# Where the norm of three feed-forwards is applied, and how SBUF is parted into pools, in a diffusion backbone step

## The chip, the core and the metric

The kernel runs on one core of one Trainium2 chip. The time is the device time of one execution in microseconds (us); lower is better. The core's engines are TensorE (PE, matrix products; PEld is its weight load), VectorE (DVE), ScalarE (ACT), GpSimd (POOL) and SyncE (SP, which issues nearly all transfers). Products accumulate in PSUM, all else lies in SBUF.

## The reference, cut to what matters

Two layers, each with a feed-forward, a mixer (attention with latent keys in layer 0, Fourier mixing in layer 1) and a second feed-forward. So there are four feed-forwards: (layer, position) = (0, 0), (0, 1), (1, 0), (1, 1). Each works on 640 tokens of 1024 features; 512 of them are sample tokens and 128 are prompt tokens, with modulations of their own.

```python
def _rms(x, g):
    y = xf * lax.rsqrt(jnp.mean(xf * xf, axis=-1, keepdims=True) + EPS)
    return (y * g).astype(x.dtype)
def _modulate(h, shift, scale):
    return h * (1 + scale) + shift
def _swiglu(h, wg, wu, wd):
    return (jax.nn.silu(h @ wg) * (h @ wu)) @ wd
...
for l in range(DEPTH):
    m = split(silu(cond) @ w_mod[l] + b_mod[l], 9)
    y = y + 0.5 * m[2] * _swiglu(_modulate(_rms(y, norm_g[l, 0]), m[0], m[1]), ffn_wg[l, 0], ffn_wu[l, 0], ffn_wd[l, 0])
    y = y + m[5] * mixer(_modulate(_rms(y, norm_g[l, 1]), m[3], m[4]))
    y = y + 0.5 * m[8] * _swiglu(_modulate(_rms(y, norm_g[l, 2]), m[6], m[7]), ffn_wg[l, 1], ffn_wu[l, 1], ffn_wd[l, 1])
```

The inner width of a feed-forward is 2816, which is 22 tiles of 128.

## The kernel before, in words

x is kept transposed: features on the 128 partitions (8 tiles d of 128 features, the k-tiles of a product), tokens along the free axis. Tokens are parted into half A (384 sample tokens) and half B (128 sample and 128 prompt tokens). A number is split into a high and a low part, and every product is made in three passes (L295 to L297 in `mm3`: high by high, low by high, high by low). Weights arrive by transfers of 512 KB that SP issues (L97, `raw`), ACT makes the high part (L101, `whi`), POOL the low part (L104, `wlo`, 512 columns at a time); three units of weights are held at once.

A feed-forward (`ffn`) goes over its 22 tiles in chunks of 4, 4, 2, 4, 4, 4. Two tiles at a time, the gate and up products of half A are made for both, then those of half B for both (48 matmuls each: 8 k-tiles, gate and up, three passes), and behind the chunk the down products of half A and of half B add into x (L494). A tile's gate and up products fill a pair of PSUM banks (`bank2`, tile name s); there are two such pairs. All else in PSUM goes through four single banks (`bank`, tile name t).

The norm (`Norm`): as soon as a tile of x is there, its product with the scale is split (`scale`, L171 on ACT and L172 on DVE), so the products can start. Two more columns in half A carry the shift through the products, so half A has 386 columns there. The factor 1/rms is multiplied onto gate and up behind the products (`scaled`, L530 on DVE, twice a tile), and the bias that the two columns gave goes into silu (L539 on ACT) and the product of the two (L540 on DVE). 1/rms itself (`rstd`) is a chain: squares on ACT (L314), their sum over tiles on POOL (L317), the sum over partitions as matmuls with ones (L333), a power on POOL (L343), three or two diagonal tiles on DVE (L350), matmuls that spread it over the partitions (L355), a copy to SBUF on ACT (L359).

The modulations of layer 1 and the last ones of layer 0 are reduced on DVE (L403) while the feed-forwards run; they need the silu of the condition in `crow`, which a transfer (L1246) and ACT (L1247) make ready after the attention. The Fourier mixer needs small tables `fc` (transfer L1019, first used at L1024).

The order of the work is the order in which the Python code emits it, engine by engine. Tasks (`spawn`, `tick`) put chains such as `rstd` and the modulations between the products: a task yields pauses in nanoseconds of PE time, and is emitted further once that much product work was emitted behind it. Memory comes from pools; a new tile waits for the readers of the old one in its place.

## Time and profile before

| | us |
|---|---|
| median of 3 runs | 2341.88 (2341.56 to 2344.65) |
| span of the profiled execution, first to last instruction | 2338.8 |
| PE busy in it | 2291.2 (98%) |
| DVE, POOL, ACT busy | 1522.5, 932.3, 769.6 |

The profiled execution has no time of its own beside its span; the median lies 3.1 us above the span. PE is busy nearly all the time, so the end of the program moves when PE does fewer or shorter matmuls, or when it waits more or less; an engine that is busy 65% of the time matters where PE waits for it.

### The profile page before, as it was taken

What the parts mean: (1) busy time and instruction counts of PE and PEld (TensorE: products, weight loads), DVE (VectorE), ACT (ScalarE), POOL (GpSimd) and SP (SyncE); (2) the same over time, 40 slices, a digit from 0 to 9 for tenths busy, and PEclk for the clock granted to TensorE, in tenths of its full rate; (3) what the DMA queues carried; (4) which work ended last, traced back from release to release, by engine and by line L of the source; (5) the groups of instructions that cost most, each with busy time, mean ns of one, the idle gap of its engine ahead of it and who ended that gap; (6) DMA issues with size and microseconds to landing.
All of it is one profiled execution on the core that took longest, in us unless ns stands there. A gap on an engine that the chain in (4) does not pass through costs nothing.

```text
span 2338.8 us, 38924 instructions
## 1 busy us (share of the span) xinstructions
PE 2291.2 (98%) x15724; PEld 2267.9 (97%) x15724; DVE 1522.5 (65%) x2852; ACT 769.6 (33%) x1601; POOL 932.3 (40%) x759
## 2 busy tenths in 40 slices
PE   8899999999999999999999999999999999999998
PEld 6899999999899999999999999999999999999998
DVE  5977778767677776777677767775356743353434
ACT  4222223253544632222224322222237422232323
POOL 1544434464111344353445543533346433343433
PEclk9999999999999999999999999999999999999999
DMA  8543434421011233344333333433212222221221
GB/s 303 167 135 127 142 121 153 135 81 55 28 42 41 91 100 127 127 136 131 131 127 100 109 127 127 144 121 103 73 51 82 71 75 73 73 76 65 94 65 46
DMA packets 70467, 243.92 MB, mean 104 GB/s; under 512 B 7888, under 2 KB 12688, under 8 KB 70032
## 3 DMA queue, kind: packets, MB, share of 16 engines
q1 hardware_dynamic: 70288, 241.44, 31.0%
q8 instruction: 124, 2.03, 0.4%
q14 instruction: 55, 0.45, 0.1%
HBM read 238.62 MB, written 2.79 MB: 103 GB/s over the span
## 4 chain that ended last, share of the span: by engine, by line
PE 89%; DVE 6%; ACT 3%; DMA 1%; issue 1%; POOL 1%; SPq 0%; POOLq 0%; DVEq 0%; ACTq 0%
PE s L296 17%; PE s L297 17%; PE s L295 17%; PE t L295 12%; PE t L296 11%; PE t L297 11%; DVE junk L403 1%; ACT whi L101 1%; DVE b L540 1%; PE t L861 0%; DVE b L305 0%; ACT p L809 0%; DVE a L305 0%; DVE x L494 0%; DVE p L812 0%
## 5 line engine op out<-in xcount | busy, mean ns | idle before, releaser
L104 POOL TENSOR_TENSOR wlo<-raw,whi 128x512 fp32r<-128x512 f32 x592 | 827.4, 1427 | 1236.8 <-ACT whi L101 1187.8
L101 ACT CAST whi<-raw 128x1024 fp32r<-128x1024 f32 (+1 forms) x303 | 306.3, 1036 | 644.9 <-PE t L296 334.9
L295 PE MATMUL s<-a,whi 128*128 128x386 f32 (+1 forms) x1408 | 478.1, 340 | 4.4 <-DVE b L530 3.3
L297 PE MATMUL s<-a,wlo 128*128 128x386 f32 (+1 forms) x1408 | 478.7, 340 | 0.1
L296 PE MATMUL s<-a,whi 128*128 128x386 f32 (+1 forms) x1408 | 478.5, 340 | 0.0
L295 PE MATMUL s<-b,whi 128*128 128x256 f32 (+1 forms) x1408 | 395.7, 281 | 0.0
L296 PE MATMUL s<-b,whi 128*128 128x256 f32 (+1 forms) x1408 | 395.5, 281 | 0.0
L297 PE MATMUL s<-b,wlo 128*128 128x256 f32 (+1 forms) x1408 | 395.4, 281 | 0.0
L494 DVE SCALAR_TENSOR_TENSOR x<-t,mod,x 128x128 f32<-128x128 f32 (+1 forms) x696 | 277.8, 433 | 160.5 <-PE t L297 157.1
L403 DVE CUSTOM_DVE_ANT_0 junk<-wmt,crow 128x1024 f32<-128x1024 f32 x256 | 372.4, 1455 | 3.5 <-ACT crow L1247 1.0
L295 PE MATMUL t<-a,whi 128*128 128x384 f32 (+1 forms) x968 | 329.8, 341 | 14.3 <-DVE x L494 5.4
L296 PE MATMUL t<-a,whi 128*128 128x384 f32 (+1 forms) x968 | 328.0, 339 | 1.3 <-DVE a L305 1.2
L297 PE MATMUL t<-a,wlo 128*128 128x384 f32 (+1 forms) x968 | 327.2, 338 | 0.0
L295 PEld LDWEIGHTS s<-a,whi 128*128 128x128 f32 x1408 | 266.8, 190 | 5.7 <-issue 4.1
L295 PE MATMUL t<-b,whi 128*128 128x256 f32 x936 | 265.2, 283 | 4.8 <-ACT b L359 2.7
L297 PEld LDWEIGHTS s<-a,wlo 128*128 128x128 f32 x1408 | 266.4, 189 | 2.2 <-issue 1.6
L296 PEld LDWEIGHTS s<-a,whi 128*128 128x128 f32 x1408 | 266.6, 189 | 1.6 <-issue 1.2
L295 PEld LDWEIGHTS s<-b,whi 128*128 128x128 f32 x1408 | 265.6, 189 | 0.0
L296 PEld LDWEIGHTS s<-b,whi 128*128 128x128 f32 x1408 | 265.5, 189 | 0.0
L297 PEld LDWEIGHTS s<-b,wlo 128*128 128x128 f32 x1408 | 265.2, 188 | 0.0
L530 DVE TENSOR_TENSOR a<-s,a 128x384 f32<-128x384 f32 x176 | 89.8, 551 | 266.3 <-ACT gub L526 264.2
L297 PE MATMUL t<-b,wlo 128*128 128x256 f32 x936 | 263.1, 281 | 0.0
(216 smaller groups left out, 3431.3 us busy)
## 6 DMA issues: line engine op xcount, KB each, us to landing
raw<-in_gu SPq DMA_DIRECT2D x176, 512.0 KB, 3.7
wmt<-in_wm SPq DMA_DIRECT2D x134, 512.0 KB, 4.0
raw<-in_dn SPq DMA_DIRECT2D x88, 512.0 KB, 3.7
raw<-in_uq SPq DMA_DIRECT2D x8, 512.0 KB, 3.6
raw<-in_wo SPq DMA_DIRECT2D x8, 512.0 KB, 3.7
raw<-in_fw SPq DMA_DIRECT2D x8, 512.0 KB, 3.7
crow<-in_wm SPq DMA_DIRECT2D x6, 512.0 KB, 5.9
junk<-in_wm SPq DMA_DIRECT2D x4, 512.0 KB, 5.3
```

Of the source, the lines that this page charges most:

```text
L101: nc.scalar.copy(hi[:, c : c + e], raw[:, :e])
L104: eng.tensor_tensor(lo[:, c + o : c + o + w], raw[:, o : o + w], hi[:, c + o : c + o + w].bitcast(F32), op=ALU.subtract,)
L295: mm(out, wh, xh, start=first and i == 0, stop=False)
L296: mm(out, wh, xl, start=False, stop=False)
L297: mm(out, wl, xh, start=False, stop=last and i == end)
L403: nc.vector.tensor_tensor_reduce(self.junk, raw, self.crow[:, c * D : (c + 1) * D], 1.0, 0.0, ALU.mult, ALU.add, self.mod[l][m][:, d, c : ...
L494: self.mark = self.nc.vector.scalar_tensor_tensor(xd, ps[:, cols], gate[:, d, c : c + 1], xd, ALU.mult, ALU.add)
L530: nc.vector.tensor_tensor(t, ps[:, m * 512 : m * 512 + n], r, op=ALU.mult)
L540: nc.vector.scalar_tensor_tensor(g[:, cols], up[:, cols], bias[:, 1, c : c + 1], g[:, cols], ALU.add, ALU.mult)
```

## The change

The last three feed-forwards, (0, 1), (1, 0) and (1, 1), take a norm `PreNorm`: 1/rms is computed first, as soon as x is complete, and x is then normalised, scaled and shifted, and split, before the products. The products have 384 columns in half A, no factor and no bias behind them: silu reads PSUM at once (`gate_up_n`). The matmul that spreads 1/rms over the partitions writes one of the two bank pairs of gate and up (`k.bank2`), and DVE reads the factor from there. The sum over partitions takes the last tile's square by itself, so the matmuls with ones number 65 in place of 50. A normalised tile holds both halves in one piece.

Second, the SBUF pools are kept as two stacks, one on the left and one on the right of SBUF. Each stage closes its pools and opens new ones in the same memory, and a first write there waits for the readers of what lay there. The tiles of the modulations (`crow` among them) and those of the Fourier mixer (`fc` among them) are opened on the right, where the attention's and a feed-forward's tiles lay.

```diff
+class PreNorm:
+    def feed(self, d, H):
...
+        sq = k.add_square(None if d == KT - 1 else self.acc[H], k.xs(d, H), H)
+        self.acc[H] = [self.acc[H], sq] if d == KT - 1 else sq
...
+    def normalise(self, H):
+        k, nc = self.k, self.k.nc
+        r = yield from k.rstd(self.acc[H], H, D, True, *self.pauses[H], False, k.bank2)
+        sh, sc = (k.mod[self.l][3 * self.i + j] for j in range(2))
+        for d in range(KT):
+            while not self.open:
+                yield 200
+            if not H:
+                self.h.append((k.wide(k.hpool, "h"), k.wide(k.hpool, "h")))
+            hi, lo = (t[:, k.cols(H)] for t in self.h[d])
+            t = k.half(H, F32)
+            x = k.xs(d, H)
+            for cols, c in k.parts(H):
+                b = sh[:, d, c : c + 1]
+                nc.vector.scalar_tensor_tensor(t[:, cols], x[:, cols], sc[:, d, c : c + 1], r[:, cols], ALU.mult, ALU.mult)
+                nc.scalar.activation(hi[:, cols], t[:, cols], AF.Identity, bias=b)
+                k.mark = nc.vector.scalar_tensor_tensor(
+                    lo[:, cols], t[:, cols], b, hi[:, cols].bitcast(F32), ALU.add, ALU.subtract
+                )
+            yield 900
...
     def open_phase(self, name):
-        self.phase = self.tc.tile_pool(name=self.name(name), bufs=1)
-        return self.phase.__enter__()
+        return self.open_pool(name, 1, "right")
...
+    def gate_up_n(self, w, h, H, G):
+        nc = self.nc
+        n = NA if H == 0 else NB
+        ps = self.bank2()
...
+        g = self.half(H, F32)
+        nc.scalar.activation(g, ps[:, :n], AF.Silu)
+        nc.vector.tensor_tensor(g, ps[:, 512 : 512 + n], g, op=ALU.mult)
+        self.split(g, *(t[:, self.cols(H)] for t in G))
...
+        def to_ffn(nxt):
+            self.close_pools(len(self.stack["left"]))
+            self.open_ffn()
+            nxt.start()
...
-        nrm, nxt = nxt, Norm(self, 0, 2)
-        nxt.pauses[0] = (7500, 5500)
+        nrm, nxt = nxt, PreNorm(self, 0, 2)
         self.mla(nrm, nxt)
+        to_ffn(nxt)
         mods_on()
         mods_go()
-        nrm, nxt = nxt, Norm(self, 1, 0)
-        self.ffn(0, 1, nrm, nxt)
+        nrm, nxt = nxt, PreNorm(self, 1, 0)
+        nxt.start()
+        self.ffn_n(0, 1, nrm, nxt)
...
+        self.ffn_n(1, 0, nrm, nxt, before_fourier)
+        self.close_pools(3, "right")
+        nrm, nxt = nxt, PreNorm(self, 1, 2)
         self.fourier(nrm, nxt)
+        to_ffn(nxt)
```

What this does to the order, at the three places that matter below. In the changed program L262 to L264 are the three lines of `normalise`, L403 is the square (L314 before), L1381 the silu of `crow` (L1247), L384 to L386 the three passes (L295 to L297), L406 POOL's sum (L317), L422 the matmul with ones (L333), L713 and L714 the silu and product of `gate_up_n`, L492 a reduction (L403), L394 the low part of a split (L305). A name ends in the number of its buffer.

**From the attention to feed-forward (0, 1), on ACT.** Before, the silu of `crow` stood ahead of the first scaled tiles of x:

```order
L304 CAST b_8246<-t_9030 128x128
L1247 ACT_TABLE_LOAD
L1247 ACTIVATE crow_9305<-crow_9305 128x2048
L171 ACTIVATE a_9084<-x_84,mod_7_108 128x384
L101 CAST whi_9034<-raw_9036 128x1024
```

Now it stands behind the squares of half B and behind two of the eight normalised tiles h:

```order
L263 ACTIVATE h_9303<-a_9305,mod_6_98 128x384
L403 ACTIVATE b_9385<-x_80 128x256
L403 ACTIVATE b_9391<-x_81 128x256
L263 ACTIVATE h_9309<-a_9311,mod_6_98 128x384
L403 ACTIVATE b_9397<-x_82 128x256
L101 CAST whi_9251<-raw_9255 128x1024
L1381 ACT_TABLE_LOAD
L1381 ACTIVATE crow_9282<-crow_9282 128x2048
L263 ACTIVATE h_9315<-a_9317,mod_6_98 128x384
L263 ACTIVATE h_9321<-a_9323,mod_6_98 128x384
```

So the third tile of h waits on ACT for the transfer of `crow` and for its silu. That transfer waits, in the changed program, for the last product of the attention's output projection, whose operands lay in its memory.

**From feed-forward (0, 1) to (1, 0), on POOL and PE.** On POOL the last two sums of half B's squares before, behind one unit's four subtractions (x2 stands for two instructions):

```order
L104 TENSOR_TENSOR wlo_13686<-raw_13687,whi_13685 128x512 x2
L104 TENSOR_TENSOR wlo_13686<-raw_13689,whi_13685 128x512 x2
L317 TENSOR_TENSOR b_13904<-b_13904,b_14055 128x256
L317 TENSOR_TENSOR b_13904<-b_13904,b_14085 128x256
L104 TENSOR_TENSOR wlo_14089<-raw_14090,whi_14088 128x512 x2
```

and now the last one:

```order
L406 TENSOR_TENSOR b_13607<-b_13607,b_13723 128x256
L104 TENSOR_TENSOR wlo_13444<-raw_13445,whi_13443 128x512 x2
L104 TENSOR_TENSOR wlo_13444<-raw_13447,whi_13443 128x512 x2
L406 TENSOR_TENSOR b_13607<-b_13607,b_13747 128x256
L104 TENSOR_TENSOR wlo_13780<-raw_13781,whi_13779 128x512 x2
```

POOL's order there is nearly the same. On PE the matmuls with ones that read this sum stood, before, behind the whole first tile (48 matmuls, and three more of the second):

```order
L295 MATMUL s_14182<-a_13708,whi_13685 128x386
L296 MATMUL s_14182<-a_13709,whi_13685 128x386
L297 MATMUL s_14182<-a_13708,wlo_13686 128x386
L333 MATMUL t_14186<-ones,b_13904 128x1 x2
L295 MATMUL s_14182<-a_13708,whi_13685 128x386
```

Now they stand in the first tile, behind 13 of its matmuls:

```order
L384 MATMUL s_13820<-h_13733,whi_13380 128x384
L385 MATMUL s_13820<-h_13734,whi_13380 128x384
L386 MATMUL s_13820<-h_13733,wlo_13381 128x384
L384 MATMUL s_13820<-h_13754,whi_13380 128x384
L422 MATMUL t_13858<-ones,b_13607 128x1
L422 MATMUL t_13858<-ones,b_13771 128x1
L422 MATMUL t_13858<-ones,b_13607 128x1
L422 MATMUL t_13858<-ones,b_13771 128x1
L385 MATMUL s_13820<-h_13755,whi_13380 128x384
```

So PE meets them 38 matmuls earlier.

**The second tile of (1, 0), on DVE.** s_13917 is half B's spread 1/rms in one bank pair, s_13897 the second tile of half A in the other. The 12 rows up to the product (L714) that frees s_13897:

```order
L264 SCALAR_TENSOR_TENSOR h_13755<-b_13948,mod_0_101,h_13754 128x128 x2
L262 SCALAR_TENSOR_TENSOR b_13961<-x_78,mod_1_102,s_13917 128x128 x2
L262 SCALAR_TENSOR_TENSOR b_13974<-x_79,mod_1_102,s_13917 128x128
L264 SCALAR_TENSOR_TENSOR h_13774<-b_13961,mod_0_101,h_13773 128x128 x2
L264 SCALAR_TENSOR_TENSOR h_13797<-b_13974,mod_0_101,h_13796 128x128
L262 SCALAR_TENSOR_TENSOR b_13974<-x_79,mod_1_102,s_13917 128x128
L262 SCALAR_TENSOR_TENSOR b_13988<-x_80,mod_1_102,s_13917 128x128 x2
L264 SCALAR_TENSOR_TENSOR h_13797<-b_13974,mod_0_101,h_13796 128x128
L492 ISA junk_9283,mod_5_106<-wmt_9285,crow_9282 128x1024
L492 ISA mod_5_106 128x1
L264 SCALAR_TENSOR_TENSOR h_13803<-b_13988,mod_0_101,h_13802 128x128 x2
L714 TENSOR_TENSOR a_13998<-s_13897,a_13998 128x384
```

Between the first read of s_13917 and L714 stand 24 such instructions of half B and two reductions. Before, the two L530 that free the second tile's bank pair stood behind the reductions alone:

```order
L305 TENSOR_TENSOR a_14179<-a_14172,a_14178 128x384
L403 ISA junk_9306,mod_5_115<-wmt_9307,crow_9305 128x1024
L403 ISA mod_5_115 128x1
L403 ISA junk_9306,mod_5_115<-wmt_9308,crow_9305 128x1024
L403 ISA mod_5_115 128x1
L530 TENSOR_TENSOR a_14252<-s_14182,a_14112 128x384
```

So the work of 1/rms on half B has moved ahead of the evacuation of the second tile, and it holds a bank pair of its own meanwhile.

## Rows read from the trace of the kernel before

**Rows 1.** The page: span, busy time. Waits of PE: us in total, times, longest.

```profile
span 2338.8 us, 38924 instructions
...
PE 2291.2 (98%) x15724; PEld 2267.9 (97%) x15724; DVE 1522.5 (65%) x2852; ACT 769.6 (33%) x1601; POOL 932.3 (40%) x759
...
PE t L295 <- DVE x L494: 6.3, 8, 1.2
```

**Rows 2.** Timeline of PE: start, duration, matmul; first and last of stretches.

```profile
803.95 0.34 PE L295 MATMUL t<-a,whi 128*128 128x384 f32 x1
...
812.33 0.28 PE L295 MATMUL t<-b,whi 128*128 128x256 f32 x1
...
824.05 0.34 PE L295 MATMUL s<-a,whi 128*128 128x386 f32 x1
...
827.57 0.34 PE L297 MATMUL s<-a,wlo 128*128 128x386 f32 x1
...
1303.56 0.34 PE L296 MATMUL s<-a,whi 128*128 128x386 f32 x1
...
1309.60 0.34 PE L297 MATMUL s<-a,wlo 128*128 128x386 f32 x1
```

**Rows 3.** Timeline of PE: matmuls behind a wait; in brackets idle time and releaser.

```profile
580.86 0.39 PE L295 MATMUL t<-b,whi 128*128 128x256 f32 x1 [2.73 <-ACT b L359]
...
831.05 0.71 PE L355 MATMUL t<-dg,ones 128*128 128x128 f32 x4 [1.33 <-DVE dg L350]
```

**Rows 4.** Windows: busy time of engines; the column behind POOL is the granted clock.

```profile
575.00:580.00 5.00, 2.38 (x12) 2.06 (x12) 4.70 (x13) 2.49 (x6) 0.19 (x1) 1.00 0.18 59
580.00:585.00 5.00, 4.14 (x19) 4.14 (x20) 3.93 (x10) 2.62 (x8) 0.00 (x0) 0.66 0.09 26
...
820.00:840.00 20.00, 18.66 (x110) 18.16 (x110) 16.80 (x33) 10.35 (x28) 13.75 (x17) 1.00 0.16 54
```

**Rows 5.** Timeline of SP and ACT, around the transfer and silu of crow.

```profile
798.31 0.33 SPq L1246 DMA_DIRECT2D crow<-in_crow  x1
...
802.85 1.28 ACT L1247 ACT_TABLE_LOAD   x1 [1.27 <-DMA crow<-in_crow]
804.14 1.92 ACT L1247 ACTIVATE crow<-crow 128x2048 f32<-128x2048 f32 x1
805.96 0.60 ACT L171 ACTIVATE a<-x,mod 128x384 fp32r<-128x384 f32 x1
```

**Rows 6.** Timeline of POOL from feed-forward (0, 1) to (1, 0).

```profile
1293.84 0.74 POOL L317 TENSOR_TENSOR b<-b,b 128x256 f32<-128x256 f32 x1 [1.79 <-ACT b L314]
1294.71 5.15 POOL L104 TENSOR_TENSOR wlo<-raw,whi 128x512 fp32r<-128x512 f32 x4
1299.82 2.67 POOL L317 TENSOR_TENSOR b<-b,b 128x256 f32<-128x256 f32 x2
```

**Rows 7.** Timeline of PE there: first matmul of the first tile; the matmuls with ones.

```profile
1293.22 0.34 PE L295 MATMUL s<-a,whi 128*128 128x386 f32 x1
...
1302.94 0.50 PE L333 MATMUL t<-ones,b 128*128 128x1 f32 x4
```

**Rows 8.** Timeline of DVE there.

```profile
1293.13 0.65 DVE L172 SCALAR_TENSOR_TENSOR b<-x,mod,b 128x128 fp32r<-128x128 f32 x2
...
1295.92 4.83 DVE L172 SCALAR_TENSOR_TENSOR b<-x,mod,b 128x128 fp32r<-128x128 f32 x4 [1.10 <-ACT b L171]
1300.68 1.21 DVE L403 CUSTOM_DVE_ANT_0 junk<-wmt,crow 128x1024 f32<-128x1024 f32 x1
...
1302.80 0.56 DVE L530 TENSOR_TENSOR a<-s,a 128x384 f32<-128x384 f32 x1 [0.90 <-ACT gub L526]
```

**Rows 9.** The tile fc: its transfer, its first use, and the time to landing.

```profile
L1024 PE MATMUL t<-mod,fc x8: 170/256/256, 1764.9 to 1765.6; 128*128 128x8 f32 x8
...
L1019 SPq DMA_DIRECT2D fc<-in_dftx x1: 327/327/327, 1616.0 to 1616.0; - x1
...
DMA to landing us min/median/max: 3.5/3.5/3.5
```

More of the change, by code (lines that the diff above doesn't have):

```diff
@@ L208, in r, with __init__, finish, later @@
         return self.task[H].join()
+class PreNorm:
+    def __init__(self, k, l, i):
+        self.k, self.l, self.i = k, l, i
+        self.h = []
+        self.acc = [None, None]
+        self.task = [None, None]
+        self.feeds = [None, None]
+        self.open = False
+        self.started = False
+        self.pauses = [(3500, 3500), (4500, 4500)]
+    def feed(self, d, H):
+        k = self.k
+        if not self.started:
+            self.started = True
+            k.need_mod((self.l, 3 * self.i), (self.l, 3 * self.i + 1))
+        sq = k.add_square(None if d == KT - 1 else self.acc[H], k.xs(d, H), H)
+        self.acc[H] = [self.acc[H], sq] if d == KT - 1 else sq
+    def finish(self, H):
+        self.task[H] = self.k.spawn(self.normalise(H))
+    def later(self, H, pace=300):
+        self.feeds[H] = self.k.spawn(self.feed_all(H, pace))
+    def feed_all(self, H, pace):
+        for d in range(KT):
+            yield pace
+            self.feed(d, H)
+        self.finish(H)
+    def start(self):
+        self.open = True
+    def normalise(self, H):
+        k, nc = self.k, self.k.nc
+        r = yield from k.rstd(self.acc[H], H, D, True, *self.pauses[H], False, k.bank2)
+        sh, sc = (k.mod[self.l][3 * self.i + j] for j in range(2))
+        for d in range(KT):
+            while not self.open:
[13 more added lines that the diff above has]
+            yield 900
+    def get(self, H):
+        if self.feeds[H] is not None:
+            self.feeds[H].join()
+        self.task[H].join()
+        return [tuple(t[:, self.k.cols(H)] for t in h) for h in self.h]
 class Kern:
@@ L320, in add_square, with rstd @@
         return acc
[L322 removed]
+    def rstd(self, acc, H, dim, bcast=True, lag=6000, gap=4200, copy=True, bank=None):
         nc = self.nc
@@ L352, in rstd @@
         yield min(gap, 1500)
-        ps = self.bank()
+        ps = (bank or self.bank)()
         for j in range(nb):
@@ L608, in ffn, with ffn_n @@
             self.down(wds, gB, 1, gate, nxt if last else None)
+            u.prefetch(nf // 2)
+    def gate_up_n(self, w, h, H, G):
+        nc = self.nc
+        n = NA if H == 0 else NB
+        ps = self.bank2()
+        wh, wl = w
+        for k in range(KT):
+            for m in range(2):
+                s = slice((m * KT + k) * P, (m * KT + k + 1) * P)
+                self.mm3(ps[:, m * 512 : m * 512 + n], [((wh[:, s], wl[:, s]), h[k])], n, k == 0, k == KT - 1)
+                if (k, m) != (KT - 1, 1):
+                    self.tick(self.last)
+        g = self.half(H, F32)
+        nc.scalar.activation(g, ps[:, :n], AF.Silu)
+        nc.vector.tensor_tensor(g, ps[:, 512 : 512 + n], g, op=ALU.mult)
+        self.split(g, *(t[:, self.cols(H)] for t in G))
+        self.tick(self.last)
+    def ffn_n(self, l, i, nrm, nxt, before_last=None):
+        gm = (l, 2 if i == 0 else 8)
+        gate = self.mod[l][gm[1]]
+        u = self.units
+        for ch, nf in enumerate(CHUNKS):
+            last = ch == len(CHUNKS) - 1
+            gs = []
+            for q in range(0, nf, 2):
+                if last and q == nf - 2:
+                    self.mods_stop()
+                ws = [u.get() for _ in range(min(2, nf - q))]
+                new = [tuple(self.wide(self.gpool, "g") for _ in range(2)) for _ in ws]
+                for w, G in zip(ws, new):
+                    self.gate_up_n(w, nrm.get(0), 0, G)
+                for w, G in zip(ws, new):
+                    self.gate_up_n(w, nrm.get(1), 1, G)
+                    u.prefetch()
+                gs += new
+            wds = [u.get() for _ in range(nf // 2)]
+            self.need_mod(gm)
+            if last and before_last is not None:
+                before_last()
+            for H in range(2):
+                g = [tuple(t[:, self.cols(H)] for t in G) for G in gs]
+                self.down(wds, g, H, gate, nxt if last else None)
             u.prefetch(nf // 2)
@@ L1014, in fourier @@
         rl = []
+        early, self.bpool = self.bpool, self.open_pool("bpool", 14)
+        self.ppool = self.open_pool("ppool", 3)
         pool = self.open_phase("fourier")
@@ L1055, in fourier @@
             if t < 4:
+                if len(A1) == 7:
+                    self.bpool = early
                 hi, lo = self.tb(), self.tb()
```

52 lines of the change are left out of this document (37 added, 15 removed).

## The prediction

> **What bounds the kernel now.** I read the page first, for the span and each engine's share, and then the waits of PE, to see what a matmul waits for. PE is busy for 2291.2 of 2338.8 us [rows 1]. So nearly all of the time is the sum of the matmuls' spacing, and the rest is some waits; the largest group in the feed-forwards is the down product waiting for x (8 times, 6.3 us in all) [rows 1]. DVE (65%), POOL (40%) and ACT (33%) count only where PE meets one of their results. I then read the timeline of PE for the spacing of its matmuls [rows 2] and for what stands behind a wait [rows 3], the windows for the granted clock behind waits [rows 4], and the timelines of the other engines at the seams between stages [rows 5 to 9], since the changed order moves work just there. The median of the runs is 3.1 us above the profiled span; I work on the span and add the change to the median.
>
> **What the change removes.** (a) Two columns in half A. The spacing at 384 columns is (812.33 - 803.95)/48 = 0.1746 us; at 386 it is (827.57 - 824.05)/20 = 0.1760 in one stretch and (1309.60 - 1303.56)/34 = 0.1776 in another [rows 2]. The difference is 1.4 to 3.0 ns. There are 22 tiles x 8 k-tiles x 2 x 3 passes x 3 feed-forwards = 3168 such matmuls: 4.4 to 9.5 us; I take the middle, 7.0. The Trainium skill (TensorE: Matmul & The Clock Gate, "Wait — 56ns, not 53.3ns?") gives the spacing of a matmul as columns over 2.4 GHz and a fixed floor. By that rule two columns are worth 0.83 ns, 2.6 us in all, and the change would be 4.4 us worse than by the rows. The rows' spacing differs by more than that, and I stay with the rows.
>
> (b) PE's wait in the first tile of (0, 1) for the spread of 1/rms, 1.33 us [rows 3], and two waits of 0.48 us just ahead of it in the output projection, part of the 6.3 us: together 2.3 us. All go, since 1/rms is now wanted elsewhere.
>
> (c) The rest of those 6.3 us are the down products of the chunk of two tiles, 3.1 us in the three later feed-forwards together. They wait for DVE, and DVE does less per tile: two multiplications with 1/rms of 0.56 us [rows 8] fall away. Bounds 0 and 3.1; I take 2.0, as that relief is as large as the wait but comes earlier. Removed: 7.0 + 2.3 + 2.0 = 11.3 us. ACT and DVE save much more, but at 65% and less this moves no end by itself.
>
> **What it adds, seam by seam.** The order of the changed program is known; I put the old durations on it.
>
> *Attention to (0, 1), half A.* Count from the end of the last output projection product. `crow` can only be sent then, and ACT handles its silu ahead of the third tile of h. From issue to the start of the table load took 802.85 - 798.31 = 4.54 us, from there to the end of the silu 805.96 - 802.85 = 3.11, and a tile of 384 columns takes ACT 0.60 [rows 5]: 8.25 us. Twelve of the tile's 48 matmuls are then done, 36 are left: 36 x 0.175 = 6.3 us, and 0.4 for the low part of the first. The tile ends at 15.0, where 48 matmuls in a row take 8.4: a wait of 6.6 us. POOL gives the same by another way, since the matmuls with ones of half B wait behind two subtractions of 1.29 and six sums of 0.74 [rows 6], 7.0 us, and some start. I take 7.5, because two chains of that length must both end; bounds 6.3 and 10 (two waits behind one another).
>
> *The same, half B.* The spread 1/rms of half B holds one of two bank pairs, so the first tile of half B must wait until the second tile of half A is evacuated: silu on ACT and a product on DVE, 0.60 + 0.56 [rows 5, 8] and two handovers, 1.5 us. Then it is paced by its own tiles of h: DVE does four instructions of 128 columns per k-tile, 4 x 0.33 = 1.3 us [rows 8], against 6 matmuls of 0.118 = 0.71. Eight times the difference is 4.7; a good half of it is done while the second tile of half A runs. I take 2.0, in all 3.5; bounds 2 and 5.
>
> *(0, 1) to (1, 0), half A.* The matmuls with ones stand behind 13 matmuls of the first tile, so PE is there 13 x 0.175 = 2.3 us after it starts. POOL first makes four subtractions, 5.15 us, and then a sum, 0.74 to 1.34 (2.67 for two) [rows 6]. The subtractions start between 0.2 us behind the tile's start (when ACT's cast can) and 1.49, as in the trace (1294.71 - 1293.22) [rows 6, 7]. So 0.2 + 5.15 + 0.74 - 2.3 = 3.8 to 1.49 + 5.15 + 1.34 - 2.3 = 5.7; I take 4.4, with the early start and the longer sum. Before, the same matmuls came at 1302.94 [rows 7], after POOL had ended its sums at 1302.49, and waited for nothing.
>
> *The same, half B.* From the spread to L714, DVE has 24 instructions of 0.33 us and two reductions of 1.21 and a read-out, 7.9 + 2.6 = 10.5 us [rows 8]. PE has 33 matmuls of half A left, 5.8 us. The wait is 4.7; I take 5.0 with a little for what POOL does then; bounds 2 (the spread comes with some of the 24 already paired) and 7.5 (a rival, below).
>
> *(1, 0) to the Fourier mixer.* `fc` now lies where the feed-forward's tiles lay, and is sent after the last down product; PE's next matmul reads it. It lands 3.5 us after the issue [rows 9], with handovers 3.7; bounds 3.5 and 4.5. Before, it was issued 148.9 us ahead of its use (1764.9 - 1616.0) [rows 9].
>
> *Fourier mixer to (1, 1).* Half A's chain is covered by the second half of the mixer's output product. Half B has the bank pair's wait and the pacing as after the attention: 3.5, bounds 2 and 5.
>
> *All seams:* 15 more matmuls with ones at 0.50/4 [rows 7], 1.9 us.
>
> Sum of waits: 7.5 + 3.5 + 4.4 + 5.0 + 3.7 + 3.5 = 27.6 us.
>
> **The clock.** Behind a wait of 2.73 us (in the 5 us around it PE was busy for 2.38) the granted clock was 0.66 over the next 5 us, so 3.4 us ran at 1.2 GHz in place of 2.4: 1.7 us lost. Behind the wait of 1.33 us at 831 it stayed 1.00 [rows 3, 4]. Four of the six places wait 3.7 us or more; the two of 3.5 us are broken up into 1.5 and small pieces. So 4 x 1.7 = 6.8 us; bounds 3.4 and 10.2.
>
> **Net:** 27.6 + 1.9 + 6.8 - 11.3 = +25.0 us, a span of 2363.8 and a median of 2341.9 + 25.0 = 2366.9 us, 1.1% slower. With all low ends of the waits (19.6), 1.9 and 3.4, less 14.9, it is +10; with all high ends (37.7), 1.9 and 10.2, less 6.7, it is +43.
>
> **Rivals.**
>
> *1. The waits are covered (faster).* At 98% PE reaches a seam late, and the emission already gives each chain pauses; if the four big waits shrink below 2.3 us each, as in the places that wait 1.3 us today, the clock stays and the 11.3 us prevail. With no wait left it is 2341.9 + 1.9 - 11.3 = 2332; break-even is at 9.4 us of waits with the clock untouched. Against it: the transfer of `fc` alone is 3.7, that of `crow` 6.6, and neither has other work in front. 7%.
>
> *2. The waits come, the clock stays.* Then +18, 2360. For it: 98% busy before and behind each. Against it: rows 4. 17%.
>
> *3. POOL holds DVE in half B.* While POOL subtracted (1294.71 to 1299.86), four DVE instructions that read two tiles of SBUF took 4.83 us, 1.2 each, not 0.33, whereas one with an operand in PSUM took its 0.56 while POOL subtracted on [rows 6, 8]. Of half B's 32 instructions per seam, the 16 of L262 read 1/rms from PSUM, the 16 of L264 two SBUF tiles. If POOL subtracts throughout, that is 16 x 0.87 = 14 us per seam, of which the 24 matmuls' time in the first tile hides some; I count 5 more for each of three seams: +40, 2382. The Trainium skill (SBUF — State Buffer, "SBUF: two separate sides") says that a DVE instruction with two SBUF inputs and a POOL instruction that reads SBUF hold a pair of ports against each other for a whole instruction; the four at 1.2 us agree. Against it: at the seams the weights' buffers are full, and POOL has four subtractions in them, not a stream. 20%.
>
> *4. It cancels.* Half of the waits come, the clock falls once: about +3, 2345. 6%.
>
> **How the numbers follow.** My forecast, 2352 to 2375, has 50%; rival 2 lies within it and rival 3 above. The range 2350 to 2385 leaves out rivals 1 and 4 and some of the tails, about 2 in 10. Within 0.2% (4.7 us) is about what a measurement of this kernel can tell from no change. Faster by more 7%, within it 6%, slower 87%.
>
> **What would show it.** In the changed profile: PE idle before L385 or L422 in the first tile of (0, 1) for 6 us or more, released by ACT's L263 or POOL's sum; idle of 4 us before the matmuls with ones of (1, 0), released by POOL; of 3.7 us before L1161, released by the transfer of `fc`; waits of the first half B tile for DVE's L714 in all three feed-forwards; a granted clock near 0.66 in 5 us behind four of these; and feed-forward stretches between the seams that are shorter by 7 to 9 us in all. The prediction fails if the transfers of `crow` and `fc` are issued long before they are wanted, if the clock stays, or if DVE is much slower than 0.33 in half B.

## The result, and the profile after

The changed kernel takes 2376.74 us (median of 4 runs, 2376.21 to 2377.37) beside 2342.05 us of the kernel before (4 runs on the same chip): a ratio of 1.0146, 95% interval 1.0131 to 1.0160, or 34.7 us slower. The forecast had been 25.0 us slower. The two profiled spans differ by 36.8 us, and the readings below are made against that.

First the page of the changed kernel (span, busy time of each engine), and from the waits of PE the lines that belong to the change (us in total, times, longest):

```profile
span 2375.6 us, 38429 instructions
...
PE 2312.0 (97%) x15754; PEld 2283.4 (96%) x15754; DVE 1325.6 (56%) x2580; ACT 727.9 (31%) x1439; POOL 953.0 (40%) x743
...
PE t L422 <- POOL b L406: 7.8, 3, 4.5
PE s L384 <- DVE a L714: 6.3, 3, 3.8
PE t L1161 <- DMA fc<-in_dftx: 3.1, 1, 3.1
PE t L384 <- DVE x L583: 2.9, 3, 1.3
PE s L385 <- DVE h L264: 2.8, 5, 1.1
PE s L384 <- ACT h L263: 2.2, 3, 1.5
```

Against [rows 1], DVE is busy for 197 us less and ACT for 42 us less. None of it moves the end. PE, the engine that decides, is busy for 21 us longer although it has only 30 more matmuls in the trace, all of them with ones (15 in the program, each of which leaves two): a matmul at half clock counts as busy for twice as long (0.69 us in the rows below, where one of 384 columns took 0.34 before). Four of the six wait lines have no counterpart before. Of the first, 1.5 us belong to the output's norm, which had such a wait of 1.6 us before; the fourth is what is left of the 6.3 us wait for x.

The next rows are PE's timeline at the seams between stages: from attention to (0, 1), from (0, 1) to (1, 0), into the Fourier mixer, and from there to (1, 1). The bracket gives the idle time and what ended it:

```profile
823.65 0.45 PE L384 MATMUL s<-h,whi 128*128 128x384 f32 x1 [1.50 <-ACT h L263]
824.60 0.69 PE L385 MATMUL s<-h,whi 128*128 128x384 f32 x1 [0.51 <-DVE h L264]
826.95 0.69 PE L384 MATMUL s<-h,whi 128*128 128x384 f32 x1 [0.38 <-ACT h L263]
829.41 1.86 PE L422 MATMUL t<-ones,b 128*128 128x1 f32 x8 [1.77 <-POOL b L406]
...
1312.13 1.48 PE L422 MATMUL t<-ones,b 128*128 128x1 f32 x8 [4.50 <-POOL b L406]
1335.25 0.36 PE L384 MATMUL s<-h,whi 128*128 128x256 f32 x1 [3.80 <-DVE a L714]
...
1790.92 1.85 PE L1161 MATMUL t<-mod,fc 128*128 128x8 f32 x8 [3.09 <-DMA fc<-in_dftx]
...
1890.95 0.44 PE L385 MATMUL s<-h,whi 128*128 128x384 f32 x1 [0.77 <-DVE h L264]
1894.53 0.44 PE L384 MATMUL s<-h,whi 128*128 128x384 f32 x1 [0.32 <-ACT h L263]
1896.09 0.44 PE L385 MATMUL s<-h,whi 128*128 128x384 f32 x1 [1.12 <-DVE h L264]
```

The waits stand at the places that the prediction named, with its releasers, and at one more: the last three rows are half A in front of (1, 1), where it had none. Behind the attention they came in pieces of 1.8 us and less, where 6 us or more had been named as the sign. The windows show what followed (the column behind POOL is the granted clock):

```profile
820.00:825.00 5.00, 2.32 (x13) 1.68 (x12) 4.39 (x12) 3.09 (x7) 3.38 (x3) 0.95 0.58 210
825.00:830.00 5.00, 2.84 (x9) 1.94 (x8) 2.16 (x4) 4.42 (x7) 4.61 (x7) 0.50 0.88 305
830.00:835.00 5.00, 4.83 (x17) 4.32 (x18) 2.65 (x7) 3.77 (x6) 2.48 (x3) 0.53 0.34 117
...
1310.00:1315.00 5.00, 2.87 (x13) 2.88 (x14) 4.56 (x8) 2.68 (x4) 5.00 (x4) 0.76 0.50 175
1315.00:1320.00 5.00, 5.00 (x19) 5.00 (x18) 3.17 (x5) 0.00 (x0) 4.70 (x4) 0.56 0.30 107
...
1335.00:1340.00 5.00, 4.75 (x27) 4.78 (x28) 4.00 (x12) 1.80 (x5) 0.00 (x0) 0.66 0.02 3
1790.00:1795.00 5.00, 4.08 (x19) 4.11 (x20) 5.00 (x6) 2.25 (x10) 4.92 (x6) 0.54 0.55 182
1795.00:1800.00 5.00, 5.00 (x36) 5.00 (x36) 3.26 (x10) 3.64 (x17) 0.40 (x1) 0.77 0.41 146
```

Where the 36.8 us lie, from the first matmuls of PE's groups on PE's timeline (a stage runs from the last group of the old work to the first undisturbed group of the new; a group is a run of 96 like matmuls):

| stage (length, and from when to when) | before | after | difference | forecast |
|---|---|---|---|---|
| attention to (0, 1) | 48.4 (803.95 to 852.34) | 59.8 (804.37 to 864.21) | +11.5 | about 11 |
| (0, 1) to (1, 0) | 42.0 (1281.18 to 1323.16) | 56.8 (1291.53 to 1348.33) | +14.8 | about 13 |
| (1, 0) to the Fourier mixer | 61.7 (1752.89 to 1814.58) | 66.9 (1775.61 to 1842.49) | +5.2 | 5.4 |
| Fourier mixer to (1, 1) | 47.6 (1839.78 to 1887.35) | 55.7 (1867.65 to 1923.38) | +8.2 | 3.5 |
| the feed-forwards between the seams | | | -3.7 | -9 |
| all else | | | +0.9 | 0 |

The first three seams stand near the forecast. The last does not, and neither does the line below it: the feed-forwards gave back 3.7 us, not 9.

### The profile page after: what moved, and what is told of

Read it like the earlier page. It is cut to its first block, busy times and chain, and to the rows that moved or that the text cites. A ratio compares the mean times of both kernels' runs of the same rounds, so it can differ in the third digit from the quotient of the medians.

```text
span 2375.6 us, 38429 instructions
## 1 busy us (share of the span) xinstructions
PE 2312.0 (97%) x15754; PEld 2283.4 (96%) x15754; DVE 1325.6 (56%) x2580; ACT 727.9 (31%) x1439; POOL 953.0 (40%) x743
## 4 chain that ended last, share of the span: by engine, by line
PE 61%; DVE 2%; ACT 1%; issue 0%; POOL 0%; DMA 0%; POOLq 0%; DVEq 0%; ACTq 0%
PE s L385 13%; PE s L384 13%; PE s L386 13%; PE t L384 7%; PE t L386 7%; PE t L385 7%; DVE h L264 1%; DVE x L583 0%; DVE b L262 0%; PE t L422 0%; POOL wlo L104 0%; DVE a L1302 0%; ACT whi L101 0%; DVE a L262 0%; DMA raw<-in_fw 0%
## 5 line engine op out<-in xcount | busy, mean ns | idle before, releaser
L384 PE MATMUL s<-h,whi 128*128 128x256 f32 (+1 forms) x2112 | 658.4, 312 | 9.0 <-DVE a L714 6.3
L385 PE MATMUL s<-h,whi 128*128 128x256 f32 (+1 forms) x2112 | 658.8, 312 | 2.8 <-DVE h L264 2.8
L386 PE MATMUL s<-h,wlo 128*128 128x256 f32 (+1 forms) x2112 | 656.9, 311 | 0.0
L384 PEld LDWEIGHTS s<-h,whi 128*128 128x128 f32 x2112 | 399.5, 189 | 12.4 <-ACT h L263 5.3
L492 DVE CUSTOM_DVE_ANT_0 junk<-wmt,crow 128x1024 f32<-128x1024 f32 x256 | 405.7, 1585 | 6.0 <-DMA wmt<-in_wm 3.4
L385 PEld LDWEIGHTS s<-h,whi 128*128 128x128 f32 x2112 | 399.9, 189 | 6.1 <-DVE h L264 6.0
L583 DVE SCALAR_TENSOR_TENSOR x<-t,mod,x 128x128 f32<-128x128 f32 (+1 forms) x696 | 280.3, 434 | 222.2 <-PE t L386 217.9
L386 PEld LDWEIGHTS s<-h,wlo 128*128 128x128 f32 x2112 | 399.8, 189 | 0.0
L384 PE MATMUL t<-g,whi 128*128 128x384 f32 (+1 forms) x1056 | 327.8, 310 | 0.0
L386 PE MATMUL t<-g,wlo 128*128 128x384 f32 (+1 forms) x1056 | 327.1, 310 | 0.0
L385 PE MATMUL t<-g,whi 128*128 128x384 f32 (+1 forms) x1056 | 327.1, 310 | 0.0
L384 PEld LDWEIGHTS t<-g,whi 128*128 128x128 f32 x1056 | 198.7, 188 | 0.5 <-DVE x L583 0.5
L714 DVE TENSOR_TENSOR a<-s,a 128x384 f32<-128x384 f32 x66 | 36.8, 557 | 290.9 <-ACT a L713 290.4
L385 PEld LDWEIGHTS t<-g,whi 128*128 128x128 f32 x1056 | 198.7, 188 | 0.0
L386 PEld LDWEIGHTS t<-g,wlo 128*128 128x128 f32 x1056 | 198.7, 188 | 0.0
L384 PE MATMUL t<-a,whi 128*128 128x384 f32 (+1 forms) x440 | 151.5, 345 | 11.5 <-ACT a L393 3.7
L385 PE MATMUL t<-a,whi 128*128 128x384 f32 (+1 forms) x440 | 150.7, 343 | 1.1 <-DVE a L394 0.9
L386 PE MATMUL t<-a,wlo 128*128 128x384 f32 (+1 forms) x440 | 149.7, 341 | 0.0
L714 DVE TENSOR_TENSOR b<-s,b 128x256 f32<-128x256 f32 x66 | 27.9, 423 | 212.2 <-ACT b L713 212.2
L713 ACT ACTIVATE a<-s 128x384 f32<-128x384 f32 x66 | 32.4, 491 | 318.9 <-PE s L386 318.9
```

What stands on the lines that cost most here:

```text
L384: mm(out, wh, xh, start=first and i == 0, stop=False)
L385: mm(out, wh, xl, start=False, stop=False)
L386: mm(out, wl, xh, start=False, stop=last and i == end)
L492: nc.vector.tensor_tensor_reduce(self.junk, raw, self.crow[:, c * D : (c + 1) * D], 1.0, 0.0, ALU.mult, ALU.add, self.mod[l][m][:, d, c : ...
L583: self.mark = self.nc.vector.scalar_tensor_tensor(xd, ps[:, cols], gate[:, d, c : c + 1], xd, ALU.mult, ALU.add)
L713: nc.scalar.activation(g, ps[:, :n], AF.Silu)
```

## The experiments

Times are medians; the kernel before ran on the same chip each time, at 2342.3 to 2342.8 us. "Before" and "after" name the two kernels.

**What the two columns were worth.** Before, with 384 columns instead of 386 in half A of all feed-forwards; the shift that the two columns carried is left out.

```diff
-        n = (NA if H == 0 else NB) + (2 if H == nrm.carrier else 0)
+        n = (NA if H == 0 else NB) + (2 if H == nrm.carrier == 1 else 0)
```

> The kernel before with 384 columns in half A of the gate and up products instead of 386 (4080 matmuls; the two shift columns are left out there, and the bias is read from other columns, so the shift is missing from the result). Theory 1 (the two columns are worth what the rows of before show, and the changed kernel lost it because its moving operands lie in tiles of another shape): spacing falls from 177 to 175 ns, 4080 x 2.0 = 8 us, 2334 us (2332 to 2336). Theory 2 (the columns are worth nothing in the old layout either): 2341 to 2343 us, spacing of 384 columns at 176 ns or more.

2333.75 us (2332.75 to 2334.46), ratio 0.9960 (0.9945 to 0.9975), 9.0 us faster. It touches 4080 matmuls: 2.2 ns each on average, which is just what step (a) took, 7.0 us for the change's 3168. By feed-forward it is 1.3 to 2.6 ns. So the columns do cost about that much in the old layout, and something in the changed kernel takes it back.

**What takes it back.** Three layouts of the changed kernel's wide tiles. The first parts each into halves, h exactly 384 and 256 columns wide, g with two unused columns behind each half; the other two keep one wide tile and set successive tiles 642 or 656 columns apart, in place of 640.

```diff
-        return pool.tile([P, NT], dt, tag=tag, name=self.name(tag))
+        pad = {"h": 0, "g": 2}[tag]
+        a = pool.tile([P, NA + pad], dt, tag=tag + "A", name=self.name(tag + "A"))
+        b = pool.tile([P, NB + pad], dt, tag=tag + "B", name=self.name(tag + "B"))
+        return Two(a[:, :NA], b[:, :NB])
```

```diff
-        return pool.tile([P, NT], dt, tag=tag, name=self.name(tag))
+        return pool.tile([P, NT + 2], dt, tag=tag, name=self.name(tag))[:, :NT]
```

> The changed kernel with h and the gated products in two tiles per half instead of one tile of 640 columns (h: 384 and 256 columns exactly; gated products: 386 and 258 columns as before, of which 384 and 256 are used). Theory 1 (tile shape sets the spacing): back to 175.0 and 118.2 ns in the three feed-forwards, 4752 matmuls x 1.0 + 4752 x 0.45 = 6.9 us less, 2370 us; if only the width of the tile counts, only the down products come back, a third of it. Theory 2 (the place of the pools or the weights' side sets it): 176.0 and 118.7 ns stay, 2376 to 2377 us.

> The changed kernel, with each wide tile of the last three feed-forwards laid out 642 columns apart instead of 640 (2 columns unused), so that the halves read by the products stand where they stood in the kernel before. Nothing else changes. Theory 1 (the distance between tiles in SBUF sets the spacing of the products): in the steady part the products over 384 columns fall from 176.0 ns back to about 175.0 and those over 256 from 118.67 to about 118.2, which over some 6,000 products of 384 columns and as many of 256 is 6 + 3 us, so about 2368 us (2366 to 2371). Theory 2 (the spacing comes with one tile that both halves share, or with the later place of the memory, not with the distance): 176.0 and 118.67 stay, 2376 to 2378 us.

> The changed kernel, with each wide tile laid out 656 columns apart (16 unused columns, 2624 bytes from tile to tile) where the run with 642 columns had 2568 bytes and the changed kernel 2560. Theory 1 (any distance other than that of the changed kernel brings the spacing back): products over 384 columns stand 174.3 to 175.5 ns apart, over 256 at 117.7 to 118.5, as with 642 columns, 2367 to 2370 us. Theory 2 (only a distance that is no multiple of 64 bytes does, so that successive tiles begin at other places within 64 bytes): 176.0 and 118.67 ns, as in the changed kernel, 2375 to 2378 us.

Narrow halves gave 2374.79 us (2372.43 to 2377.53), 642 columns 2368.41 (2367.15 to 2370.39) and 656 columns 2364.01 (two runs, 2362.06 and 2365.97). The same chunk of four tiles in (0, 1) shows it without any seam: first matmul of its predecessor's down products to first matmul of its own, on PE's timeline. Before, then after:

```profile
1179.62 0.34 PE L295 MATMUL t<-a,whi 128*128 128x384 f32 x1
...
1264.38 0.34 PE L295 MATMUL t<-a,whi 128*128 128x384 f32 x1
```

```profile
1189.75 0.34 PE L384 MATMUL t<-g,whi 128*128 128x384 f32 x1
...
1274.63 0.34 PE L384 MATMUL t<-g,whi 128*128 128x384 f32 x1
```

Then before with 384 columns, and after with 656 columns from tile to tile:

```profile
1178.30 0.34 PE L295 MATMUL t<-a,whi 128*128 128x384 f32 x1
...
1262.78 0.34 PE L295 MATMUL t<-a,whi 128*128 128x384 f32 x1
```

```profile
1187.43 0.33 PE L384 MATMUL t<-g,whi 128*128 128x384 f32 x1
...
1271.38 0.34 PE L384 MATMUL t<-g,whi 128*128 128x384 f32 x1
```

That is 84.76 us before, 84.88 after, 84.48 before with fewer columns, 83.95 after with 656 columns (84.43 with 642). A chunk of four tiles has 576 matmuls, and a feed-forward is 5.5 such chunks. Between after and the run with 656 columns, chunks of (0, 1) and (1, 1) differ by 0.83 to 0.93 us, those of (1, 0) by 0.33 to 0.54: some 12 us over the three, which is nearly the whole difference of the two kernels (12.7). From matmul to matmul, gate and up in (0, 1) stand 176.00 ns (384 columns) and 118.67 ns (256 columns) apart after, 174.26 and 118.08 with 642 columns, 173.68 and 117.64 with 656 (medians over the groups of 96). In the run with halves, gate and up, read from h at 1536 and 1024 bytes from tile to tile, stayed at 176.0 and 118.7, and down, read from g at 1544 and 1032 bytes, came back to 174.7 to 174.9 in half A and 118.4 to 118.7 in half B. So it is how the tiles are laid out and not the one tile for two halves, and both halves pay for it. The distance alone does not fix it: with 642 columns the down products, which read g at the same 2568 bytes, stayed at 175.9 and 118.9 in (0, 1), while gate and up came back; with 656 both came back. A new distance also moves where each tile begins, and no run parts the two. The theory that only a distance off 64 bytes helps fell: 656 columns are 2624 bytes, a multiple of 64, and the best. Which property of 2560, 1536 and 1024 bytes does it (all are multiples of 512), and why, stays open.

**The Fourier seam.** `fc` is loaded early, in a pool of its own; in a second run the five zero tiles `rl` that DVE fills there are early as well.

```diff
-        fc = pool.tile([P, 6 * P], F32, name="fc", tag="fc")
-        nc.sync.dma_start(fc, self.io["dftx"])
+        fc, rl = self.fc, self.rl
...
-        for t in range(5):
-            r = pool.tile([P, 256], F32R if t < 4 else F32, name=f"rl{t}", tag=f"rl{t}")
-            nc.vector.tensor_copy(r, z)
-            rl.append(r)
```

> The changed kernel with the Fourier tables fc in a pool of their own that is opened, and loaded, when the last chunk of feed-forward (1, 0) begins to be emitted. Theory (wait for the transfer plus clock): the wait of 3.25 us and most of the 6.9 us at half clock behind it go, 5 to 6.5 us less, 2370.5 to 2371.5. Rival (something else is late at the same place, the normalised tiles or the weights): 0 to 3 us less, and PE idle there shows another releaser.

> The changed kernel, with both late things of the Fourier stage moved out of the memory that the feed-forward holds: the transfer of fc and DVE's five zero fills stand in a pool of their own, opened before that feed-forward. Theory 1 (T3's price is these two waits, the second behind the first): PE's wait on fc (3.1 us) and the one behind the fills, which was 5.4 us when fc alone was early, both go, and with them the clock's fall; the stretch from the last down group of the third feed-forward to the first group of the Fourier stage's end falls from 66.9 us to 61 to 63, 2370 to 2373 us. Theory 2 (a third thing waits for the same memory, or the stage is bound by DVE's evacuations): the stretch stays over 65.5 us, 2375 to 2379 us.

`fc` alone gave 2379.98 us (2378.32 to 2381.02), no gain (3.2 us more than after; in the trace the stages behind the attention and in front of (1, 1) are 1.1 and 1.6 us longer): the wait for the transfer went and another of 5.37 us came. On the timeline of DVE and PE in that run, DVE's fills of `rl` stand between L172 and the evacuations L1196 for which PE waits:

```profile
1793.82 2.62 DVE L1177 CAST rl<-fz 128x256 fp32r<-128x256 f32 x2
1796.35 0.28 DVE L1177 COPY rl<-fz 128x256 f32<-128x256 f32 x1
1796.55 0.88 DVE L1196 SCALAR_TENSOR_TENSOR b<-t,rstd,b 128x256 fp32r<-128x256 f32 x2
...
1797.08 0.58 PE L384 MATMUL t<-whi,a 128*128 128x256 f32 x1 [5.37 <-DVE qm L1238]
```

As read from this, they could not be filled while the feed-forward held the memory either; the next run bears it out. The named releaser, a memset of 0.07 us, only came last. With both early the stage took 61.66 us, as before the change (61.69), the granted clock stayed at 1.00, and the kernel took 2373.62 us (2370.47 to 2375.64). The seam's 5.2 us are these two waits, one hidden behind the other.

**POOL's sum ahead of (1, 0).** The seventh tile's sum of half B's squares goes to DVE.

```diff
-        sq = k.add_square(None if d == KT - 1 else self.acc[H], k.xs(d, H), H)
+        eng = k.nc.vector if H == 1 and d == KT - 2 and (self.l, self.i) == (1, 0) else None
+        sq = k.add_square(None if d == KT - 1 else self.acc[H], k.xs(d, H), H, eng)
```

> The changed kernel with one sum (the seventh tile of half B's squares for feed-forward (1, 0)) on VectorE instead of GpSimd, so that it no longer stands behind four subtractions. Theory: the wait of 4.5 us at the matmuls with ones falls below 1, and the clock does not fall (6.8 us at half clock cost 3.4): 5 to 7.5 us less, 2369 to 2372. Rival (the wait only moves on: the power on GpSimd and the spread of 1/rms come when they came, and half B's wait for L714 grows): 0 to 2 us less, 2375 to 2377.

2375.13 us (2375.01 to 2375.48). PE's wait before the matmuls with ones fell from 4.50 to 0.79 us, but two waits for DVE's h of 0.42 and 1.34 us came behind it, and half B's wait of 3.80 us with its fall of the clock stayed. The stage became 2 us shorter: the wait had mostly moved on.

**The pair of banks.** Half B's spread 1/rms goes to a single bank and is copied to SBUF, as before the change.

```diff
-        r = yield from k.rstd(self.acc[H], H, D, True, *self.pauses[H], False, k.bank2)
+        r = yield from k.rstd(self.acc[H], H, D, True, *self.pauses[H], H == 1, None if H else k.bank2)
```

> The changed kernel, with half B's spread 1/rms copied from its PSUM bank to SBUF and the pair of banks released, as half A does already. Theory 1 (half B's products wait in the three places because the pair of banks, or the scaling that reads it, holds them): PE's waits on L714 (3.8 us in all, the longest in the second place) and the two of 1.4 us on L264 go, and with the first the clock's fall of 1.7 us: 2370 to 2372 us. Theory 2 (half B waits for DVE's chain of scaling itself, and this now has both operands in SBUF beside POOL's subtractions, as half A has): the waits stay or grow, L264 of half B takes 1.5 us where it took 0.6, 2376 to 2381 us.

2367.31 us (2363.61 to 2368.55), 9.4 us faster than after, more than forecast. All waits on L714 are gone. After, DVE in front of (1, 0), where L714 stands behind half B's chain:

```profile
1331.80 0.86 DVE L262 SCALAR_TENSOR_TENSOR b<-x,mod,s 128x128 f32<-128x128 f32 x3
...
1334.02 0.61 DVE L264 SCALAR_TENSOR_TENSOR h<-b,mod,h 128x128 fp32r<-128x128 f32 x2
1334.55 0.55 DVE L714 TENSOR_TENSOR a<-s,a 128x384 f32<-128x384 f32 x1
```

With the copy, the same place:

```profile
1320.97 0.56 DVE L714 TENSOR_TENSOR a<-s,a 128x384 f32<-128x384 f32 x1 [2.51 <-ACT a L713]
1323.76 0.88 DVE L262 SCALAR_TENSOR_TENSOR b<-x,mod,b 128x128 f32<-128x128 f32 x3 [1.09 <-ACT b L448]
```

L714 now stands ahead of the chain and runs as soon as its silu is there; PE's waits in half B are 0.2 us and less, and the clock is 1.00 in the windows from 1320 to 1335. That a DVE instruction with both operands in SBUF would be held again did not happen: half B's L262 takes 346 ns, 341 after. POOL was idle at that time.

**POOL against DVE.** The scaled value t goes to a PSUM bank, so L264 has one operand in SBUF instead of two.

```diff
-            t = k.half(H, F32)
+            t = k.bank()[:, : NA if H == 0 else NB]
```

> The changed kernel, with the scaled value t (the first of the three steps that make h) written to a PSUM bank instead of SBUF. Theory 1 (DVE's L264, h = t times the modulation plus the shift, is slow only because it and POOL's subtractions both work on SBUF operands): with its big operand in PSUM it takes 0.6 to 0.8 us where it took 1.6 to 3.1 beside POOL; the first group of half A in front of (1,1) falls from 23.1 us to 17 to 19, that of (0,2) by 1 to 3 of its 27, that of (1,0) by about 1: 2368 to 2371 us. Theory 2 (DVE is only late, not held): L264 stays over 1.2 us, or the banks' release takes the place of the wait: 2376 to 2382 us.

2377.21 us (2375.46 to 2379.67), no gain. The groups of DVE by line and shape, after and then with PSUM (count, busy time, mean ns of one):

```profile
L264 DVE SCALAR_TENSOR_TENSOR h<-a,mod,h 128x384 fp32r<-128x384 f32 x24 | 21.7, 917 | 3.0 <-ACT h L263 2.8
L264 DVE SCALAR_TENSOR_TENSOR h<-b,mod,h 128x128 fp32r<-128x128 f32 x48 | 15.2, 350 | 1.2 <-ACT h L263 1.2
```

```profile
L264 DVE SCALAR_TENSOR_TENSOR h<-t,mod,h 128x128 fp32r<-128x128 f32 x48 | 15.1, 347 | 5.8 <-ACT h L263 5.8
L264 DVE SCALAR_TENSOR_TENSOR h<-t,mod,h 128x384 fp32r<-128x384 f32 x24 | 13.8, 611 | 7.8 <-ACT h L263 7.5
```

The holding of L264 is real (917 against 611 ns) and sits in half A alone. The trace after shows it too: the seven L264 of half A during which POOL does nothing take 0.61 us each, the other 17 up to 1.70; L262, with one operand in SBUF, takes 0.60 beside POOL and without:

```profile
L262 DVE SCALAR_TENSOR_TENSOR a<-x,mod,s 128x384 f32<-128x384 f32 x24 | 14.0, 603 | 4.0 <-PE s L444 4.0
```

The run gained little by it: the first group in front of (1, 1) fell from 23.1 to 21.9 us, as DVE still comes to h late. It did not take all of the holding away there: the evacuation L1273, which this run did not change, takes 0.28 us without POOL and up to 1.33 beside its subtractions, and its mean over 16 of 128 columns rose from 489 to 567 ns. So what the holding costs in that seam was not measured. In front of (1, 0) that group fell from 30.3 to 21.9, but there the order of the program had moved too: the matmuls with ones stand 30 matmuls into the first tile instead of 13 and wait for nothing. Half B's use of the banks cost nearly all of it back: 2.8 to 2.9 us in each of three groups, waits for ACT's h.

**The seam behind the attention.** Half B's six sums go to DVE, and the silu of `crow` is made to follow half A's last h.

```diff
+        eng = k.nc.vector if H == 1 and (self.l, self.i) == (0, 2) else None
...
+            z = self.small(1)
+            nc.vector.tensor_scalar(z, nrm.h[KT - 1][1][:, 0:1].bitcast(F32), 0.0, None, ALU.mult)
+            nc.scalar.activation(self.crow, self.crow, AF.Silu, bias=z)
```

> The changed kernel, with two things out of the way in front of (0,2) alone: half B's six sums of squares are made by DVE instead of POOL, and the silu of the row of modulations (with its load of a function table) is held behind half A's last h on ACT. Theory 1 (the 7.8 us wait there is made of POOL's sums for the ones-products, 1.8 us, and of ACT's copies of h standing behind table load and silu, 1.5 us and 0.7 us, with a half-speed clock behind them): the first group of half A falls from 27.0 us to 18 to 21, 2369 to 2372 us. Theory 2 (DVE's own chain of 1/rms, scale and multiply is what is last there, and now gets the six sums as well): the group stays over 24 us, 2374 to 2378 us.

2372.11 us (2371.59 to 2373.52): 4.6 us of gain, less than theory 1 had. The first group fell from 27.0 to 23.2 us. Here too the matmuls with ones moved, from 7 to 54 matmuls into the half, so it stays open how much is the sums, the silu or that place. A wait of 1.50 us for the first h remains, the clock still falls, and the chunk of two takes 1.5 us longer: all waits of PE for x there and elsewhere grew from 2.9 to 5.2 us.

**All together.** Copy, t in PSUM for half A alone, sums and silu, early `fc` and `rl`, with 642 columns; and then with 656 columns and the sum of the fourth experiment.

```diff
-            t = k.half(H, F32)
+            t = k.half(H, F32) if H else k.bank()[:, :NA]
```

> The changed kernel with what the other runs point to, together: wide tiles 642 columns apart; half B's spread 1/rms copied to SBUF; half A's scaled value t in a PSUM bank (half B's stays in SBUF); in front of (0,2) half B's six sums on DVE and the silu held behind half A's h; fc and the zero fills early. If the gains stand apart and add up: 8.3 (distance of the tiles) + 9.4 (copy) + about 4 (t in PSUM, what is left of it in the second and the last place once the copy is made) + 4.6 (sums and silu) + about 5 (Fourier stage) = 31 us, 2345 us, so just behind the kernel before. If the waits of half A and half B are one chain seen twice, so that the gains overlap: 2350 to 2358 us. If taking them all away keeps the clock up too: 2336 to 2342 us, faster than the kernel before.

> All six mends together, as in the run before, with the wide tiles 656 columns apart instead of 642, and for (1,0) the seventh tile's sum of half B's squares on DVE. Theory 1 (the gains of the distance hold on top of the others): 2343.4 less the 4.4 us by which 656 columns beat 642 and less 0 to 1.6 us for the sum = 2337.4 to 2339 us, faster than the kernel before by 3 to 5 us. Theory 2 (with all mends in, DVE is so full in front of (1,0) that the sum costs as much as it frees, and part of the distance's gain was the run's own spread): 2341 to 2344 us, no change against before.

2343.42 us (2342.32 to 2345.71, 11 runs), ratio 1.0007 (0.9998 to 1.0016): 33.3 us less than after, where the sum forecast had 31. So the gains do not overlap. But the mends had brought only 25 us when each was measured alone (8.3, 9.4, none, 4.6 and 3.1); which of them is worth more beside the others was not measured. In its trace the clock falls behind the attention alone, not in the other seams. The last version took 2341.42 us (2339.52 to 2342.41, 11 runs), ratio 0.9994 (0.9985 to 1.0003): not told apart from the kernel before, and 2.0 us below the version with 642 columns, within the range of its second theory. No run beats the kernel before but the first, which leaves the shift out.

## Why the prediction was right or wrong

The direction and the cause held: the change trades work on engines that have time for waits on the one that has none. The size was 10 us short. Of the 11.8 us by which the spans exceed the forecast, 5.3 lie in the feed-forwards, some 5 in the clock and 1.4 in the matmuls with ones; the waits together came out near their sum.

**Columns (a), forecast 7.0 us gained, measured about nothing.** This is the step that failed. In the old layout its 2.2 ns per matmul were confirmed on average (9.0 us over 4080). But the new tiles lie 2560 bytes apart, and that layout costs up to 2.3 ns per matmul of 384 columns and 1.0 of 256: some 12 us, going by the run with 656 columns. The prediction took the old spacing at 384 columns from the output projection [rows 2] and carried it to tiles that lay elsewhere. The Trainium skill's formula, columns over 2.4 GHz and a fixed floor (TensorE: Matmul & The Clock Gate, "Wait — 56ns, not 53.3ns?"), knows no distance of tiles either: it would give one spacing where the runs show 173.7 to 176.0 ns at 384 columns and the full clock. The relief of two columns is real, but the new layout took about as much back.

**Chunks of two (c), forecast 2.0.** They gave 2.1 and 2.1 in two feed-forwards and -0.1 in the third, 4.1 in all and above the bound of 3.1. They are all of the -3.7.

**The matmuls with ones, forecast 1.9, measured 3.3.** Four rows in the trace are two matmuls, so one costs 0.22 us and not 0.50/4.

**The seams.** Half A behind the attention: PE idle for 2.8 us in the group and 1.5 ahead of it, 4.3 against 7.5 (6.7 by the starts of the matmuls, which count some of the slower clock). Of the two named chains POOL's sums are the long wait, 1.77 us. `crow`'s silu ran ahead of the third h as foreseen, but ACT did not wait for the transfer: it came to the table load 7.5 us after the issue (at 820.6), behind its own squares and h. The next wait of PE was one of 0.17 us:

```profile
828.15 1.28 ACT L1381 ACT_TABLE_LOAD   x1
829.45 1.91 ACT L1381 ACTIVATE crow<-crow 128x2048 f32<-128x2048 f32 x1
831.26 2.12 ACT L263 ACTIVATE h<-a,mod 128x384 fp32r<-128x384 f32 x4
...
833.58 0.69 PE L385 MATMUL s<-h,whi 128*128 128x384 f32 x1 [0.17 <-DVE h L264]
```

(1, 0): 4.5 and 3.8 us against 4.4 and 5.0. `fc`: 3.1 against 3.7. Half B behind attention and Fourier mixer, by the starts: one wait of 1.4 us and 2.2 us of small ones in each, 3.6 against 3.5.

**Half A behind the Fourier mixer, forecast 0, measured 3.2 us by the starts.** "Covered" failed: DVE has the cover's own work to do, the evacuations of the output product (L583, L1273), which stand between its L264. Its L264 there was held besides. Beside four subtractions of POOL, it took 1.70 us, and two in a row 3.09:

```profile
1884.27 5.53 POOL L104 TENSOR_TENSOR wlo<-raw,whi 128x512 fp32r<-128x512 f32 x4 [1.60 <-ACT whi L101]
...
1885.68 1.70 DVE L264 SCALAR_TENSOR_TENSOR h<-a,mod,h 128x384 fp32r<-128x384 f32 x1
1887.31 0.60 DVE L583 SCALAR_TENSOR_TENSOR x<-t,mod,x 128x128 f32<-128x128 f32 x2
1887.83 2.06 DVE L1273 TENSOR_SCALAR x<-x,cfb 128x128 f32<-128x128 f32 x2
...
1893.10 5.65 POOL L104 TENSOR_TENSOR wlo<-raw,whi 128x512 fp32r<-128x512 f32 x4 [1.61 <-ACT whi L101]
...
1894.51 3.09 DVE L264 SCALAR_TENSOR_TENSOR h<-a,mod,h 128x384 fp32r<-128x384 f32 x2 [0.47 <-ACT h L263]
```

The two L1273 beside POOL's subtractions took 2.06 us, where one takes 0.28 without. How much of the 3.2 us is such holding and how much the evacuations themselves stays open; with t in PSUM the group was 1.2 us shorter. Rival 3 had the mechanism, but put it in half B, where POOL is idle and L264 takes its 350 ns. The rule of the Trainium skill behind it (SBUF — State Buffer, "SBUF: two separate sides"), that a DVE instruction with two SBUF inputs and a GpSimd instruction that reads SBUF lock each other out, agrees with the PSUM run: one SBUF operand fewer, 611 ns in place of 917. Rival 4's sum was wrong: half of the waits, the ones and one fall of the clock, less 11.3, are +6, not +3.

**The clock, forecast 6.8, measured some 12 us.** The clock fell behind the four waits that were counted, but three of the falls cost more than 1.7 us. In a window of 5 us the loss is at most 5 times one less the granted clock: 0.25 + 2.5 + 2.35 behind the attention, 1.2 + 2.2 and then 1.7 in front of (1, 0), 2.3 + 1.15 in the Fourier mixer, 13.6 us in all. PE stood idle for some 2.8 us of that time, which already count as waits, so 12 are left. Behind the attention, where waits follow one another, the clock was 1.2 GHz for some 10 us; behind the waits of 4.50 and 3.09 us it was so for nearly 7, although PE was busy from then on; behind that of 3.80 for 3.4, as in the model. That model was one row [rows 4], and its upper bound, 10.2, was too low as well.

That the first two seams came out near the forecast all the same is partly luck: the larger loss of clock stands against less waiting than forecast, 4.3 us against 7.5 and 8.3 against 9.4. Step (b) took 2.3 us from the old price; before, the stretch behind the attention had 1 to 1.5 us of smaller delays besides, and in that at (1, 0) PE waited for nothing.

## What to carry to other kernels

When a change gives tiles another size or place, the spacing of the instructions that read them is a term of its own: compare it in undisturbed stretches of both traces before explaining anything by waits. Work moved from behind the products to ahead of them is paid at each seam where PE is the bound: name for each what DVE, ACT and POOL still have in their queues there, and do not price the clock by one row: here a fall cost from 1.7 to 5 us. A wait that is removed alone shows the next one (`fc`, then `rl`; POOL's sum, then L264): the worth of a mend is known when the stage, not the wait, is shorter.
